# The last column of a ConvFFN: where two ScalarE copies and two VectorE taps stand among the prompt's taps

## The chip, the cores and the metric

The kernel runs on one core of a Trainium2 chip. The metric is the device time of one execution in microseconds; the time of a kernel is the median over its timed executions. A core has five engines that work through queues of their own and meet through semaphores: TensorE (PE, matrix products into PSUM), VectorE (DVE), ScalarE (ACT), GpSimd (POOL) and SyncE (SP, which only issues transfers here). Matrices lie in SBUF and accumulators in PSUM, both 128 partitions wide; large tensors and scratch lie in HBM.

## The reference

One layer of a diffusion backbone on 128 prompt tokens and 1024 sample tokens (a grid of 16 by 64), width 1024: adaLN modulation, a mixer of gated linear attention heads, and a ConvFFN, each with a residual, then a final norm. The change lies in the ConvFFN:

```python
def dw_conv(u, conv_w, conv_b, grid):      # depthwise: 3x3 over the grid, or width 3 over the prompt
    ...
    return out + conv_b

def conv_ffn(h, w_up, conv_w, conv_b, w_down, grid):
    u = dw_conv(h @ w_up, conv_w, conv_b, grid)
    gate, up = jnp.split(u, 2, axis=-1)
    return (jax.nn.silu(gate) * up) @ w_down
```

`w_up` is 1024 x 5632, `w_down` 2816 x 1024, all in float32.

## The kernel before, in words

**Products.** Every float32 operand is split into a high part (a rounded copy, written by ScalarE) and a low part (the rest, a subtraction). One product is then three matmuls: high by high, high by low, low by high. The large products are arranged as seven products of half matrices in place of eight.

**Up stage.** The 2816 hidden channels are 22 columns of 128 (c = 0 to 21), each with a gate half and an up half. For a column PE fills two PSUM tiles `u` (128 channels by 1024 sample tokens, gate and up), and a tile `x` with the prompt's values, which it turns round at the end (`turn_prompt`, L2085). The convolution writes `acc[c][0]` (gate) and `acc[c][1]` (up), 1152 tokens wide: the middle tap with the bias is one ACT instruction for the sample tokens (`conv_middle`, L1964) and one for the prompt (`prompt_middle`, L1994); the other eight taps of the grid (`gate_tap`, `up_tap`, L1982) and the two of the prompt (`prompt_tap`, L2002) are multiply-adds on DVE. Then ACT takes the Silu of the gate (L2131 in the last column), POOL multiplies gate by up (L2172) and the result is stored to the scratch `scr_g`, of which POOL also makes sums (`late`, L1924 to L1928) that are stored to `scr_s`. A column's taps run on DVE while PE works on the next column. Of the last column (c = 21, `last_rest`) three gate taps run inside the loop, and 13 taps of the grid and four of the prompt come behind.

**Down stage.** It is seven products over 11 pairs of columns (j = 0 to 10) each. For a pair, SP loads tokens and weights, 512 columns each, into one raw tile of 128 x 1024 (L129, two transfers), ACT writes the high part (`wuh` or `wh`), and an engine the low part (`wul` or `wl`, a subtraction): in the first product POOL does this for pairs 0 to 6 and DVE for pairs 7 to 10, later DVE for all. A pair is 12 matmuls (four tiles of 128 tokens, three each, L2439); the first three pairs of the first product are taken together, 36 matmuls. Each pair needs both parts; there are seven places for parts and six raw tiles, taken in rotation, so that a place is written again when PE has read it, and a raw tile is loaded again when its low part has been made. In the listings L254 and L133 are the same copy of `load_w`, L254 and L69 the same subtraction; which line is shown depends on who called it.

**What sets the order.** The framework places the instructions on each engine; `tc.issue_after(x)` says that what is made under it stands behind x on its engine. Three chains matter. `vec` strings DVE's taps, prompt taps and the low parts of pairs 7 to 10 one behind the other in the order in which they are written. `InTurn(nc.scalar, "pair_high")` strings ACT's high parts of pairs 1 to 6, starting behind the last column's last copy out of PSUM. `InTurn(nc.gpsimd, "pair_low")` does so for POOL's low parts. An engine executes its queue strictly in order, and SP's loads are a queue too.

Of the kernel before, what the change touches and what calls it, by code (L numbers as in the profile page):

```python
# [49 lines left out]
def kernel(ctx: ExitStack, tc: tile.TileContext, ins, outs, stop=None):  # L50
# [11 lines left out]
    anchor = {}  # L62
# [5 lines left out]
    def split_lo(eng, out, full, hi):  # L68
        return eng.tensor_tensor(out, full, hi.bitcast(F32), op=ALU.subtract)  # L69
# [37 lines left out]
    def turn(key):  # L107
        slots["n"] += 1
        return slots[key][slots["n"] // 2 % len(slots[key])]

    def next_raw():
        slots["raws"].append(slots["raws"].pop(0))
        return slots["raws"][-1]

    def load_w(srcs, shape, eng, high=nc.scalar):

        if slots["fixed"]:
            raw = next_raw()
            hi, lo = slots["fixed"].pop(0)
            slots["fixed"].append((hi, lo))  # L120
        else:
            wp = turn("w")
            raw = turn("raw").tile([P] + shape, F32, name="raw", tag="raw")
            hi = wp["h"].tile([P] + shape, F32R, name="wh", tag="wh")
            lo = wp["l"].tile([P] + shape, F32R, name="wl", tag="wl")
        if isinstance(srcs, (list, tuple)):
            n = shape[-1] // len(srcs)
            for i, src in enumerate(srcs):
                anchor["load"] = nc.sync.dma_start(raw[..., i * n : (i + 1) * n], src)  # L129
        else:  # L130
            anchor["load"] = nc.sync.dma_start(raw, srcs)
        def split():
            high.activation(hi, raw, AF.Copy)  # L133
            split_lo(eng, lo, raw, hi)

        if slots["hold"]:
            slots["held"].append(split)
        else:
            split()
        return hi, lo  # L140
# [122 lines left out]
    def load_pair(p, j):  # L263
        a, b = PRODUCTS[p](j)
        if p > 1:
            return load_w([a, b], [2 * 512], nc.vector)
        low = InTurn(nc.gpsimd, "pair_low") if j < 7 else InTurn(nc.vector, "vec")
        return load_w([a, b], [2 * 512], low, InTurn(nc.scalar, "pair_high") if 0 < j < 7 else nc.scalar)

    def seq_product(p):  # L270
        for j in range(NPAIR):
            seq.append((1, lambda j=j: load_pair(p, j)))
# [1244 lines left out]
    def turn_prompt():  # L1517

        for q in range(2):
            pt = turned["p", q] = ps_p.tile([P, 4, P], F32, name="x", tag="x")  # L1520

            def fn():
                for j in range(4):
                    kt = 4 * q + j
                    last = nc.tensor.transpose(pt[:, j, :], xns[8][:, kt * P : (kt + 1) * P], ident)
                return last

            run("pe", fn)
# [432 lines left out]
    def conv_middle(u, ch, acc, ra=0, rb=NROW):  # L1961

        bc = vcol[:, col["conv_b"] + ch : col["conv_b"] + ch + 1]
        return nc.scalar.activation(  # L1964
            acc[:, ra * GRID : rb * GRID],
            u[:, ra * GRID : rb * GRID],
            AF.Identity,
            bias=bc,
            scale=convc[:, 4 * 44 + ch : 4 * 44 + ch + 1],
        )  # L1970

    def conv_rest(u, ch, acc, ra=0, rb=NROW, part=slice(0, 8)):

        wc = lambda t: convc[:, t * 44 + ch : t * 44 + ch + 1]
        u3 = u.rearrange("p (r c) -> p r c", c=GRID)
        a3 = acc[:, 0:NS].rearrange("p (r c) -> p r c", c=GRID)
        taps = [(dy, dx) for dy in (-1, 0, 1) for dx in (-1, 0, 1) if dy or dx]
        for dy, dx in taps[part]:
            r0, r1 = max(ra, -dy), min(rb, NROW - dy)
            c0, c1 = max(0, -dx), min(GRID, GRID - dx)  # L1980
            o = a3[:, r0:r1, c0:c1]
            last = nc.vector.scalar_tensor_tensor(  # L1982
                o,
                u3[:, r0 + dy : r1 + dy, c0 + dx : c1 + dx],
                wc(3 * (dy + 1) + dx + 1),
                o,
                op0=ALU.mult,
                op1=ALU.add,
            )
        return last  # L1990

    def prompt_middle(pp, ch, acc):
        bc = vcol[:, col["conv_b"] + ch : col["conv_b"] + ch + 1]
        return nc.scalar.activation(  # L1994
            acc[:, NS:NT], pp, AF.Identity, bias=bc, scale=convc[:, 4 * 44 + ch : 4 * 44 + ch + 1]
        )
# [26 lines left out]
    def up(c, p, kts=range(4)):  # L2023

        if p in (2, 3, 5):
            Z, Y = u[c][0][:, 0:512], u[c][0][:, 512:NS]
        else:
            X = u[c][1][:, 0:512]
        chained(
            {  # L2030
                1: lambda: up_product(X, c, "11", "b11", True, False),
                2: lambda: up_product(Z, c, "12", "b21", True, True),
                3: lambda: up_product(Y, c, "s4", "b22", False, True, kts),
                4: lambda: up_product(X, c, "22", "t4", False, True),
                5: lambda: up_product(Y, c, "s1", "t1", True, False),
                6: lambda: up_product(X, c, "s2", "t2", False, False),
                7: lambda: up_product(X, c, "s3", "t3", False, False),
            }[p]
        )
        if p == 5 and c:  # L2040
            copy(c, "p5", Y)
        elif p == 1:
            copy(c, "p1", X)
        elif p == 6:
            copy(c, "u2", X)
# [24 lines left out]
    def vec(fn):  # L2070
        with tc.issue_after(anchor["vec"].ins) if "vec" in anchor else nullcontext():
            anchor["vec"] = fn()

    def gate_tap(c, i):
        vec(lambda: conv_rest(u[c][0], c, acc[c][0], part=slice(i, i + 1)))

    def up_tap(c, i):
        vec(lambda: conv_rest(u[c][1], 22 + c, acc[c][1], part=slice(i, i + 1)))
# [38 lines left out]
    def last_rest(c):  # L2117

        up(c, 4)
        gate_p, up_p = turn_prompt(c)  # L2120
        prompt_middle(*gate_p)
        prompt_middle(*up_p)
        for dx in (-1, 1):
            prompt_tapped(gate_p, dx)
            prompt_tapped(up_p, dx)
        last = conv_middle(u[c][1], 22 + c, acc[c][1])
        with tc.issue_after(last.ins):
            nc.scalar.dma_start(scr_g[c - 1], gs[c - 1])
        for i in range(3, 8):
            gate_tap(c, i)  # L2130
        nc.scalar.activation(acc[c][0], acc[c][0], AF.Silu)  # L2131
        for i in range(8):
            up_tap(c, i)
        second_gate(c)

    def prompt_tapped(pp, dx):
        vec(lambda: prompt_tap(*pp, dx))
# [27 lines left out]
    def second_gate(c):  # L2165

        accg, accu = acc[c]
        if c not in FIXED:
            with after("p1") if c == 0 else nullcontext():
                nc.scalar.activation(accg, accg, AF.Silu)  # L2170
        gs[c] = accg
        last = anchor["gate"] = nc.gpsimd.tensor_tensor(accg, accg, accu, op=ALU.mult)  # L2172
        if c + 1 not in FIXED or c not in FIXED:
            nc.gpsimd.dma_start(scr_g[c], accg)
        if sums_todo and c > 0:
            with tc.issue_after(last.ins):
                sums_todo.pop(0)()
        if c % 2 == 1:
            token_sums(c // 2)
# [7 lines left out]
    for c in range(NHID + 1):  # L2187
# [26 lines left out]
        if c == NHID:  # L2214
            last_rest(c - 1)
        elif c - 1 in FIXED:
            fixed_rest(c - 1)
        elif c > 0:
            taps = prompt_columns(c - 1)
            up(c - 1, 4)  # L2220
            second_half(c - 1)
# [370 lines left out]
```

## Time and profile before

| | |
|---|---|
| three timed executions | 1503.16, 1504.57 and 1507.5 us; median 1504.57 |
| the profiled execution | 1507.08 us, of which the span of the program's instructions is 1505.3 us |
| granted TensorE clock over the span | 0.996 |
| busy in the span | PE 1459.9 us (97%), DVE 1135.9 (75%), ACT 783.1 (52%), POOL 700.6 (47%) |
| the up stage | from about 811 us to 1253.7 us of the span |
| the down stage | from 1253.7 us to the end |

The times in the rows are microseconds from the start of the span. In a row of the timeline stand the start, the duration, the engine (with a q where it is the sequencer that issues a transfer), the line, the operation, what it writes and reads, the shape, and the number of instructions merged in the row; in brackets the idle time ahead of it and what ended that. Neighbouring instructions of one engine overlap by about 0.1 us, so durations of single instructions add up to a little more than the stretch they fill. Matmuls are listed with their full latency (0.39 us), while they start 0.23 us apart.

### The profile page before, as it was taken

Reading aid. Unit: us, or ns where it says so; the run is one execution under the profiler, and the core shown is the slowest. Engines: PE = TensorE matmul, PEld = TensorE weight load, DVE = VectorE, ACT = ScalarE, POOL = GpSimd, SP = SyncE. Lnnn points to the kernel's source line nnn. Section 1 sums busy time; section 2 is a strip of 40 time slices with the busy share of each in tenths; the row PEclk is TensorE's granted clock in tenths of the full one; section 3 lists DMA queues with packets and bytes.
Section 4 is the critical chain, followed back from the end, with each engine's and each line's share of the span. In section 5 each row is a group of like instructions: output and inputs, shape, how many; then the busy total and the mean of one; then the engine's idle time right before and its main releaser. Section 6 shows DMA issues by size and latency. Waiting matters only on the chain.

```text
span 1505.3 us, 31115 instructions
## 1 busy us (share of the span) xinstructions
PE 1459.9 (97%) x12509; PEld 1250.9 (83%) x12509; DVE 1135.9 (75%) x1727; ACT 783.1 (52%) x1524; POOL 700.6 (47%) x524
## 2 busy tenths in 40 slices
PE   6999999999999999899999999999999999999998
PEld 2899998999898999777788888888888887888886
DVE  3766565565565777755799999999999999689475
ACT  3575667555455555622674454444444444466444
POOL 1602122324332241222329999999999996100001
PEclk9999999999999999999999999999999999999999
DMA  9411121335525454867662555545654567979752
GB/s 338 139 44 48 41 61 54 113 91 172 175 77 190 134 165 160 308 238 256 208 193 79 180 166 143 151 115 145 197 134 125 170 167 232 362 257 372 237 192 116
DMA packets 173803, 253.80 MB, mean 169 GB/s; under 512 B 11828, under 2 KB 113698, under 8 KB 171738
## 3 DMA queue, kind: packets, MB, share of 16 engines
q1 hardware_dynamic: 150455, 173.52, 35.9%
q0 software_dynamic: 20000, 66.99, 15.0%
q10 hardware_dynamic: 3203, 11.30, 2.0%
q8 instruction: 98, 1.61, 0.4%
q14 instruction: 47, 0.39, 0.1%
HBM read 191.93 MB, written 82.90 MB: 183 GB/s over the span
## 4 chain that ended last, share of the span: by engine, by line
PE 80%; DMA 6%; DVE 4%; ACT 3%; POOL 3%; issue 3%; SPq 0%; POOLq 0%; DVEq 0%; ACTq 0%
PE u L1798 24%; PE mm L642 15%; PE xb L2439 7%; PE yb L2439 6%; PE mm L656 5%; PE x L2056 4%; PE mm L794 3%; PE lv L981 3%; PE yb L2493 2%; PE u L1562 2%; PE x L1049 2%; PE mm L536 1%; DMA raw<-in_w_in_dram 1%; DMA wa<-in_w_ada_dram 1%; PE ada L1218 1%
## 5 line engine op out<-in xcount | busy, mean ns | idle before, releaser
L1982 DVE SCALAR_TENSOR_TENSOR acc<-u,convc,acc 128x945 f32<-128x945 f32 (+2 forms) x352 | 425.2, 1217 | 6.0
L69 POOL TENSOR_TENSOR wl<-raw,wh 128x1024 fp32r<-128x1024 f32 x40 | 97.8, 2448 | 251.5 <-ACT wh L133 199.0
L642 PE MATMUL mm<-h1h,wh 128*128 128x384 f32 x528 | 185.0, 350 | 0.6 <-ACT qj L545 0.6
L642 PE MATMUL mm<-h1h,wl 128*128 128x384 f32 x528 | 179.0, 339 | 0.0
L642 PE MATMUL mm<-h1l,wh 128*128 128x384 f32 x528 | 179.0, 339 | 0.0
L944 DVE TENSOR_TENSOR Q<-Q,fb 128x384 f32<-128x384 f32 x126 | 82.7, 656 | 85.2 <-PE lv L981 84.4
L69 POOL TENSOR_TENSOR wul<-sr,wuh 128x512 fp32r<-128x512 f32 (+1 forms) x62 | 112.8, 1820 | 11.0 <-ACT wuh L1780 8.4
L69 POOL TENSOR_TENSOR wul<-ra,wuh 128x1024 fp32r<-128x1024 f32 (+1 forms) x43 | 109.1, 2539 | 15.7 <-ACT wuh L1780 15.7
L934 ACT ACTIVATE m<-k 128x384 f32<-128x384 f32 x126 | 70.2, 557 | 82.2 <-DVE k L946 38.7
L2403 POOL TENSOR_TENSOR sq<-sq,mhalf 128x1 f32<-128x1 f32 x9 | 10.8, 1199 | 204.5 <-DVE sq L2402 204.5
L642 PEld LDWEIGHTS mm<-h1h,wh 128*128 128x128 f32 x528 | 99.5, 188 | 5.5 <-issue 3.9
L642 PEld LDWEIGHTS mm<-h1l,wh 128*128 128x128 f32 x528 | 99.5, 188 | 0.6 <-issue 0.2
L642 PEld LDWEIGHTS mm<-h1h,wl 128*128 128x128 f32 x528 | 99.3, 188 | 0.8 <-issue 0.5
L656 PE MATMUL mm<-wh,h1h 128*128 128x256 f32 x288 | 83.9, 291 | 1.5 <-ACT v L681 1.5
L946 DVE TENSOR_TENSOR k<-k,fb 128x384 f32<-128x384 f32 x126 | 74.2, 589 | 12.2 <-ACT m L934 7.2
L656 PE MATMUL mm<-wh,h1l 128*128 128x256 f32 x288 | 80.5, 280 | 0.0
L656 PE MATMUL mm<-wl,h1h 128*128 128x256 f32 x288 | 80.5, 279 | 0.0
L133 ACT ACTIVATE wh<-raw 128x1024 fp32r<-128x1024 f32 x48 | 50.8, 1058 | 42.5 <-PE mm L642 11.8
L2172 POOL TENSOR_TENSOR acc<-acc,acc 128x1152 f32<-128x1152 f32 x22 | 60.5, 2751 | 8.8 <-DVE acc L1982 7.7
L2018 ACT ACTIVATE u2p<-u 128x512 f32<-128x512 f32 x44 | 26.4, 599 | 69.4 <-PE u L1798 68.3
L1780 ACT ACTIVATE wuh<-ra 128x1024 fp32r<-128x1024 f32 (+1 forms) x43 | 44.3, 1034 | 34.6 <-POOL acc L2172 18.4
L1780 ACT ACTIVATE wuh<-sr 128x512 fp32r<-128x512 f32 (+1 forms) x63 | 48.8, 774 | 22.2 <-PE x L2056 16.6
(402 smaller groups left out, 4467.4 us busy)
## 6 DMA issues: line engine op xcount, KB each, us to landing
ra<-in_w_ffn_up_dram SPq DMA_DIRECT2D x84, 256.0 KB, 3.4
raw<-in_w_in_dram SPq DMA_DIRECT2D x32, 512.0 KB, 4.7
v<-in_w_ada_dram SPq DMA_DIRECT2D x27, 512.0 KB, 4.4
scr_s<-late POOLq DMA_DIRECT2D x11, 1024.0 KB, 6.0
scr_t<-in_w_ffn_down_dram POOLq DMA_DIRECT2D x16, 704.0 KB, 8.5
scr_g<-acc ACTq DMA_DIRECT2D x18, 576.0 KB, 3.8
wa<-in_w_ada_dram SPq DMA_DIRECT2D x16, 512.0 KB, 6.2
scr_t<-in_w_ffn_down_dram POOLq DMA_DIRECT2D x2, 2816.0 KB, 12.3
```

Of the source, the lines that this page charges most:

```text
L69: return eng.tensor_tensor(out, full, hi.bitcast(F32), op=ALU.subtract)
L642: anchor["fill"] = mm(ps, a[:, kt, :], h[kt][b], start=(n == 0), stop=(n == 23))
L656: anchor["fill"] = mm(ps, h[kt][t // 3][:, ts_], a[:, kt % 4, :], start=(n == 0), stop=(n == 23))
L934: nc.scalar.activation(aps(t, 0, [[2 * h, NB], [h, 2], [1, h]]), aps(src, 0, [[2 * h, NB], [BL + h, 2], [1, h]]), AF.Copy)
L944: nc.vector.tensor_tensor(qm, qm, aps(ff_, 2 * h - 1, [[BL - h, 2], [2 * h, NB], [0, h]]), op=ALU.mult)
L946: nc.vector.tensor_tensor(km, km, aps(ff_, BL + 2 * h - 1, [[-(BL + h), 2], [2 * h, NB], [0, h]]), op=ALU.mult)
L1780: return lambda: nc.scalar.activation(hi, raw, AF.Copy), lambda eng: split_lo(eng, lo, raw, hi)
L1798: last = mm(dst, w_slot(c, a, x)[:, kt, :], HB[y][b][:, kt, :], start=(start and n == 0), stop=(stop and n == 11), skip_group_check=True,)
L1982: last = nc.vector.scalar_tensor_tensor(o, u3[:, r0 + dy : r1 + dy, c0 + dx : c1 + dx], wc(3 * (dy + 1) + dx + 1), o, op0=ALU.mult, op1=AL ...
L2056: last = mm(pk, HB[h]["p"][:, 4 * half + kt, :], aps(flat(W[x]), a * 512 + kt * P, [[(b - a) * 512, 2], [1, P]]), start=(half + kt + n == ...
L2172: last = anchor["gate"] = nc.gpsimd.tensor_tensor(accg, accg, accu, op=ALU.mult)
L2439: anchor["down"] = mm(banks[i][:, cs], w[a][:, ts_], w[b][:, 512 + cs.start : 512 + cs.stop], start=(start and j == 0 and n == 0), stop=(j ...
```

## The change

Two edits. In `load_pair` the high part of the sixth pair (j = 5), and through the chain that of the seventh, now stands on ACT behind the last column's second prompt middle, where before the chain only ran behind the fifth pair's. In `last_rest` the gate taps 3 and 4 stand ahead of the four prompt taps on DVE, where before they stood behind them. No instruction is added or removed, and no shape changes.

```diff
@@ load_pair
         a, b = PRODUCTS[p](j)
         if p > 1:
             return load_w([a, b], [2 * 512], nc.vector)
+        if j == 5:
+            anchor["pair_high"] = anchor["last_middle"]
         low = InTurn(nc.gpsimd, "pair_low") if j < 7 else InTurn(nc.vector, "vec")
         return load_w([a, b], [2 * 512], low, InTurn(nc.scalar, "pair_high") if 0 < j < 7 else nc.scalar)
@@ last_rest
         gate_p, up_p = turn_prompt(c)
         prompt_middle(*gate_p)
-        prompt_middle(*up_p)
+        anchor["last_middle"] = prompt_middle(*up_p)
+        gate_tap(c, 3)
+        gate_tap(c, 4)
         for dx in (-1, 1):
             prompt_tapped(gate_p, dx)
             prompt_tapped(up_p, dx)
         last = conv_middle(u[c][1], 22 + c, acc[c][1])
         with tc.issue_after(last.ins):
             nc.scalar.dma_start(scr_g[c - 1], gs[c - 1])
-        for i in range(3, 8):
+        for i in range(5, 8):
             gate_tap(c, i)
```

On PE and SP every instruction stands where it stood. The first place is ACT at the turn from the up stage to the down stage: `wh0`, `wh1`, `wh2` are the high parts of pairs 4, 5 and 6, `acc0` and `acc1` up and gate of the last column, L1964 and L1994 the middle taps of the sample tokens and of the prompt, `scr_g20` the store of the column before. Before:

```order
L254 ACTIVATE wh0_14092<-raw0_14098 128x1024
L254 ACTIVATE wh1_14094<-raw1_14099 128x1024
L254 ACTIVATE wh2_14096<-ra_10292 128x1024
L1964 ACTIVATE acc0_9782<-u_13954,vcol_212,convc_8784 128x1024
L1994 ACTIVATE acc1_10299<-x_14037,vcol_212,convc_8784 128x128
L1994 ACTIVATE acc0_9782<-x_14037,vcol_212,convc_8784 128x128
L2128 DMA scr_g20_139<-acc3_10300 128x1152
L2131 ACTIVATE acc1_10299<-acc1_10299 128x1152
```

and in the changed kernel, whose line numbers behind L266 are two to four higher:

```order
L254 ACTIVATE wh0_14092<-raw0_14098 128x1024
L1966 ACTIVATE acc0_9782<-u_13954,vcol_212,convc_8784 128x1024
L1996 ACTIVATE acc1_10299<-x_14037,vcol_212,convc_8784 128x128
L1996 ACTIVATE acc0_9782<-x_14037,vcol_212,convc_8784 128x128
L254 ACTIVATE wh1_14094<-raw1_14099 128x1024
L254 ACTIVATE wh2_14096<-ra_10292 128x1024
L2132 DMA scr_g20_139<-acc3_10300 128x1152
L2135 ACTIVATE acc1_10299<-acc1_10299 128x1152
```

The two high parts and the three middle taps have changed places; the issue of the store now stands behind the high parts.

The second place is POOL in the same stretch, where the low parts `wl0`, `wl1`, `wl2` of pairs 4 to 6 stand beside one of the sums for `scr_s` (`late`). Before:

```order
L254 TENSOR_TENSOR wl0_14093<-raw0_14098,wh0_14092 128x1024
L254 TENSOR_TENSOR wl1_14095<-raw1_14099,wh1_14094 128x1024
L1927 TENSOR_TENSOR late_10480<-acc3_10300 128x512
L254 TENSOR_TENSOR wl2_14097<-ra_10292,wh2_14096 128x1024
L2172 TENSOR_TENSOR acc1_10299<-acc1_10299,acc0_9782 128x1152
```

and in the changed kernel:

```order
L254 TENSOR_TENSOR wl0_14093<-raw0_14098,wh0_14092 128x1024
L1929 TENSOR_TENSOR late_10480<-acc3_10300 128x512
L254 TENSOR_TENSOR wl1_14095<-raw1_14099,wh1_14094 128x1024
L254 TENSOR_TENSOR wl2_14097<-ra_10292,wh2_14096 128x1024
L2176 TENSOR_TENSOR acc1_10299<-acc1_10299,acc0_9782 128x1152
```

The sum has moved ahead of the sixth pair's low part.

The third place is DVE, from the last gate tap that runs inside the loop (the first row) to the first up taps. Before:

```order
L1982 SCALAR_TENSOR_TENSOR acc1_10299<-u_13876,convc_8784,acc1_10299 128x15x63
L2002 SCALAR_TENSOR_TENSOR acc1_10299<-x_14037,convc_8784,acc1_10299 128x127
L2002 SCALAR_TENSOR_TENSOR acc0_9782<-x_14037,convc_8784,acc0_9782 128x127
L2002 SCALAR_TENSOR_TENSOR acc1_10299<-x_14037,convc_8784,acc1_10299 128x127
L2002 SCALAR_TENSOR_TENSOR acc0_9782<-x_14037,convc_8784,acc0_9782 128x127
L1982 SCALAR_TENSOR_TENSOR acc1_10299<-u_13876,convc_8784,acc1_10299 128x16x63 x2
L1982 SCALAR_TENSOR_TENSOR acc1_10299<-u_13876,convc_8784,acc1_10299 128x15x63
L1982 SCALAR_TENSOR_TENSOR acc1_10299<-u_13876,convc_8784,acc1_10299 128x960
L1982 SCALAR_TENSOR_TENSOR acc1_10299<-u_13876,convc_8784,acc1_10299 128x15x63
```

and in the changed kernel:

```order
L1984 SCALAR_TENSOR_TENSOR acc1_10299<-u_13876,convc_8784,acc1_10299 128x15x63
L1984 SCALAR_TENSOR_TENSOR acc1_10299<-u_13876,convc_8784,acc1_10299 128x16x63 x2
L2004 SCALAR_TENSOR_TENSOR acc1_10299<-x_14037,convc_8784,acc1_10299 128x127
L2004 SCALAR_TENSOR_TENSOR acc0_9782<-x_14037,convc_8784,acc0_9782 128x127
L2004 SCALAR_TENSOR_TENSOR acc1_10299<-x_14037,convc_8784,acc1_10299 128x127
L2004 SCALAR_TENSOR_TENSOR acc0_9782<-x_14037,convc_8784,acc0_9782 128x127
L1984 SCALAR_TENSOR_TENSOR acc1_10299<-u_13876,convc_8784,acc1_10299 128x15x63
L1984 SCALAR_TENSOR_TENSOR acc1_10299<-u_13876,convc_8784,acc1_10299 128x960
L1984 SCALAR_TENSOR_TENSOR acc1_10299<-u_13876,convc_8784,acc1_10299 128x15x63
```

The row of two taps, 3 and 4, has moved ahead of the four prompt taps.

## The prediction

> **What bounds the kernel now.** I read the page first (PE busy 97% of the span), then the chain of waits, which runs over PE almost throughout, then what PE waited for from the end of the up stage to the end of the kernel:
>
> ```profile
> PE xb L2439 <- DVE wul L254: 2.2, 1, 2.2
> PE yb L2439 <- DVE e L2388: 0.6, 1, 0.6
> ```
>
> Columns: who waited for whom, microseconds in total, times, longest. In the last 250 us PE waits twice. The change can touch only the first wait. PE's timeline around it:
>
> ```profile
> 1272.64 0.39 PE L2439 MATMUL xb<-wh,wl 128*128 128x512 f32 x1
> 1272.87 0.39 PE L2439 MATMUL xb<-wuh 128*128 128x512 f32 x1
> 1275.46 0.50 PE L2439 MATMUL xb<-wul,wuh 128*128 128x512 f32 x1 [2.21 <-DVE wul L254]
> ...
> 1276.97 0.63 PE L2439 MATMUL xb<-wul,wuh 128*128 128x512 f32 x1
> ...
> 1280.37 0.39 PE L2439 MATMUL xb<-wuh 128*128 128x512 f32 x1
> ...
> 1287.85 0.39 PE L2439 MATMUL yb<-wh 128*128 128x512 f32 x1
> ```
>
> At 1272.87 the eighth pair (j = 7) begins; its second matmul needs the low part, the first that DVE makes, and gets it at 1275.46. From 1276.97 to 1280.37 matmuls take 0.63 us in place of 0.39. The pace without either is 0.227 us, from the chain of waits, where 132 matmuls take 29.92 us:
>
> ```profile
> 1288.01 29.92 PE yb L2439 x132
> ```
>
> Four pairs (j = 7 to 10, 48 matmuls) thus need 48 x 0.2267 = 10.88 us; they took 1287.85 - 1272.87 = 14.98. Lost: 4.10 us, of which 1275.46 - 1273.10 = 2.36 is the wait and 1.74 the slow matmuls. Why DVE is late:
>
> ```profile
> 1250.30 3.68 DVE L1982 SCALAR_TENSOR_TENSOR acc<-u,convc,acc 128x945 f32<-128x945 f32 x3
> 1257.03 1.12 DVE L2002 SCALAR_TENSOR_TENSOR acc<-x,convc,acc 128x127 f32<-128x127 f32 x4 [3.04 <-ACT acc L1994]
> 1258.06 16.22 DVE L1982 SCALAR_TENSOR_TENSOR acc<-u,convc,acc 128x1008 f32<-128x1008 f32 x13
> 1274.20 1.21 DVE L254 TENSOR_TENSOR wul<-ra,wuh 128x1024 fp32r<-128x1024 f32 x1
> 1275.33 5.94 DVE L254 TENSOR_TENSOR wul<-sr,wuh 128x1024 fp32r<-128x1024 f32 x2
> ```
>
> After three gate taps DVE idles 3.04 us for ACT's prompt middles, then runs without a gap to pair 7's low part (1274.20 to 1275.41), and PE starts 0.05 us later. So DVE's idle time is what ends PE's wait. ACT in that stretch:
>
> ```profile
> 1252.25 2.00 ACT L254 ACTIVATE wh<-raw 128x1024 fp32r<-128x1024 f32 x2
> 1254.15 1.05 ACT L254 ACTIVATE wh<-ra 128x1024 fp32r<-128x1024 f32 x1
> 1254.98 0.33 ACTq L2128 DMA_DIRECT2D scr_g<-acc  x1
> 1255.10 1.20 ACT L1964 ACTIVATE acc<-u,vcol,convc 128x1024 f32<-128x1024 f32 x1
> 1256.19 0.80 ACT L1994 ACTIVATE acc<-x,vcol,convc 128x128 f32<-128x128 f32 x2
> 1264.44 1.17 ACT L2131 ACTIVATE acc<-acc 128x1152 f32<-128x1152 f32 x1 [7.45 <-DVE acc L1982]
> ```
>
> **ACT's part.** The middles stand behind three high parts. Their inputs are ready earlier: the end of PE's up column.
>
> ```profile
> 1253.35 0.39 PE L1798 MATMUL u<-t4h,wul 128*128 128x512 f32 x1
> 1253.58 0.38 PE L2085 MATMUL x<-ident,late 128*128 128x128 f32 x2
> ```
>
> `u` is complete at 1253.74, the turned prompt at 1253.96. With `wh1` and `wh2` behind them, ACT is free when `wh0` ends, 1252.25 + about 1.05 = 1253.3. So the sample middle starts at 1253.77 and the prompt middles end 1.9 us later (1255.10 to 1256.99 now), at 1255.7. That is 1.3 us earlier.
>
> **DVE's part.** The two taps need no prompt middle. They run in the idle time: 1253.98 + 2 x 1.25 (16.22 / 13) = 1256.5. There the prompt middles have been ready for 0.8 us. The four prompt taps follow (1258.06 - 1257.03 = 1.03 us), then 11 taps. All of the 3.04 us goes, so every DVE instruction from the 11 taps on shifts by 3.04: pair 7's low part runs from 1271.16 to 1272.38. PE wants it at 1272.87 + 0.23 = 1273.10, so 0.7 us to spare. What is late next is pair 8's low part. SP reloads a raw tile at once when its low part is made, which shows the ends of the single instructions, and POOL's row shows why pair 8's is slow:
>
> ```profile
> 1275.44 0.32 SPq L129 DMA_DIRECT2D ra<-scr_g  x1
> 1279.03 0.32 SPq L129 DMA_DIRECT2D sr<-scr_g  x1
> 1281.30 0.32 SPq L129 DMA_DIRECT2D sr<-scr_g  x1
> 1283.53 0.32 SPq L129 DMA_DIRECT2D raw<-scr_g  x1
> ```
>
> ```profile
> 1274.42 3.50 POOL L2172 TENSOR_TENSOR acc<-acc,acc 128x1152 f32<-128x1152 f32 x1 [7.71 <-DVE acc L1982]
> ```
>
> Pair 8's took 3.7 us (1275.33 to 1279.0) and ended 1.08 us after POOL's gate product (1277.92), about the length of one such instruction: it seems to have stood until POOL was through. POOL's product waits for DVE's last tap, so both shift together and the delay stays. Shifted by 3.04, pair 8 ends at 1275.96, pair 9 at 1278.24, pair 10 at 1280.47. Without the wait PE wants them at 1273.10 + 2.72 per pair: 1275.82, 1278.54, 1281.26. So about 0.15 us of a new wait at pair 8, none behind it. From the next product on DVE was ahead already: at 1290.20 it made the low part of that product's sixth pair (j = 5), which PE wants at 1283.9 + 5 x 2.72 + 0.23 = 1297.7 even when it is four microseconds earlier.
>
> ```profile
> 1290.20 1.21 DVE L69 TENSOR_TENSOR wul<-raw,wuh 128x1024 fp32r<-128x1024 f32 x1
> 1293.73 1.23 DVE L69 TENSOR_TENSOR wul<-raw,wuh 128x1024 fp32r<-128x1024 f32 x1 [2.32 <-ACT wuh L133]
> ```
>
> Its seventh pair's is done at 1294.96, wanted at 1300.4. The loads behind these also move, since most are released by DVE; unmoved they would still do.
>
> **POOL, SP and the store.** What stands behind the moved instructions:
>
> ```profile
> 1257.96 5.13 POOL L254 TENSOR_TENSOR wl<-raw,wh 128x1024 fp32r<-128x1024 f32 x2
> 1262.68 1.66 POOL L1927 TENSOR_TENSOR late<-acc 128x512 f32<-128x512 f32 x1
> 1263.94 2.78 POOL L254 TENSOR_TENSOR wl<-ra,wh 128x1024 fp32r<-128x1024 f32 x1
> ```
>
> ```profile
> 1260.76 0.33 SPq L129 DMA_DIRECT2D raw<-scr_g  x1
> ```
>
> `wh1` and `wh2` now end at about 1256.6 and 1257.6, 2.4 us later, but POOL takes up `wl1` only after 1260.3. The sum ahead of it costs 1.26 us (1262.68 to 1263.94): `wl1` ends at 1264.4 in place of 1263.1, `wl2` at 1266.7 as before. PE wants them at 1267.65 and 1270.37 (24 and 12 matmuls ahead of pair 7, and one), so 3.3 and 3.7 us to spare: cost nothing, one raw reload 1.3 us later. The store of `scr_g20` is issued at 1257.5, not 1254.98. Pair 10's load at 1260.76 waits for it. How long transfers that touch `scr_g` take to land, and the loads of `raw` from it:
>
> ```profile
> DMA to landing us min/median/max: 1.9/2.9/10.0
> ...
> raw<-scr_g SPq DMA_DIRECT2D x6, 256.0 KB, 4.6
> ```
>
> With 2.9 the store lands at 1260.4, with 10.0 at 1267.5, and SP's queue would stand for 6.7 us. Pair 10's high part is wanted at 1281.0. A load takes 4.6 us, ACT 1.05: even then it is ready at about 1273.2. Nothing, with bounds of 0 on both sides. The Silu follows tap 7 and moves 3 us ahead, and so do the high parts behind it.
>
> **The slow matmuls.** Stretches of one length, PE's busy time first, the granted clock third from the end:
>
> ```profile
> 386.05:389.46 3.41, 1.88 (x61) 1.15 (x59) 0.00 (x0) 0.47 (x1) 1.00 (x1) 1.00 0.57 157
> 628.39:631.81 3.42, 1.59 (x54) 1.12 (x54) 2.91 (x9) 2.16 (x8) 0.05 (x1) 1.00 1.02 413
> 631.81:635.22 3.41, 3.41 (x25) 2.37 (x28) 2.04 (x6) 2.43 (x6) 1.50 (x2) 0.50 1.01 407
> 1273.51:1276.93 3.42, 1.47 (x6) 1.24 (x7) 3.42 (x3) 0.00 (x0) 2.51 (x1) 1.00 0.38 128
> 1276.93:1280.34 3.41, 3.41 (x9) 2.67 (x8) 3.41 (x2) 1.06 (x1) 3.01 (x4) 0.50 0.63 239
> ```
>
> Twice a stretch of 3.41 us in which PE idled 53 to 57% is followed by one at half the clock; one with 45% idle (386.05) shows none. I take it that the wait brings the half clock, and without the wait the 1.74 us goes too. The Trainium skill ("TensorE: Matmul & The Clock Gate", section "Why this matters for your kernels") puts the limit at idle gaps of more than about 3 us; by it 2.2 us would bring no half clock and 1.74 us would stay. The row of 1276.93 speaks against it.
>
> **The sum,** against the profiled execution (1507.08): -2.36 + 0.15 - 1.74 = -3.95, so 1503.1. The median of the timed executions is 2.5 below that execution, so it had less of such losses. If the 3.41 us grid lies anywhere, 2.21 us of idle time puts half a window (1.71) into one with (1.20 + 2 x 0.50) / 3.41 = 65% of its positions. For a typical execution I count 0.65 x 1.74 = 1.1, in all -2.2 - 1.1 = -3.3: 1504.57 - 3.3 = 1501.2. A change under 0.3% (4.5 us) is about what a measurement here cannot tell from none.
>
> **The rivals.**
> 1. The half clock has another cause, or was not in the median execution: only the wait goes, -2.2, so 1502.4. For it: the median is 2.5 us below the profiled time. Against it: the rows above. The skill's rule belongs here.
> 2. POOL's product starts ahead of pair 7's low part and DVE stands behind it. Both are released by the same tap; now DVE is 0.22 us ahead (1274.20 against 1274.42). The other way round the low part ends at 1271.3 + 2.7 + 1.1 = 1275.1, PE still waits 2.0 us, the half clock stays: about -0.3, so 1504.3. That POOL's product took 3.50 us here speaks for such blocking, but the order is by the tap's end, and stays. The Trainium skill ("SBUF — State Buffer", "SBUF: two separate sides") has it that whichever of the two starts first keeps the port for its whole instruction.
> 3. The change doesn't do what it says: the middles are not earlier (ACT held by something else). Then the taps alone fill 2.5 of the 3.04 us, DVE shifts by 2.5, pair 7 is in time still and pair 8 0.7 us late: -1.7 - 1.1, 1501.8. Within the forecast's range.
> 4. Slower: the store. From a landing after 1281.0 - 4.6 - 1.05 = 1275.3 (18 us after issue) on, pair 10's high part is late and PE waits microsecond for microsecond. To lose the gain of 3.3 and 4.5 us more it must land at about 1283, 26 us after issue: 1509.1 and more. Against it: the longest was 10.0 us.
>
> **How the numbers follow.** Forecast 0.75 (with rival 3, 0.06 of it), rival 1 0.13, rival 2 0.08, rival 4 0.04. The forecast's saving lies between 2.2 and 3.95, so 1500.6 to 1502.4; the three timed executions lie 4.3 us apart, a median of three scatters by some 1.5 us, so its own range is 1498.4 to 1503.4. The range takes in part of rival 2: 1498.2 to 1504.0. Faster by over 0.3% means below 1500.06, 1.1 below the forecast: some 0.4 of the forecast, 0.15 of rival 1, in all 0.32. Slower by over 0.3%: rival 4, 0.04. Within: 0.64.
>
> **What would show it.** Right: no idle time on DVE ahead of the prompt taps; the second matmul of pair 7 0.23 us after the first; at most 0.3 us of waiting at pair 8; the clock 1.00 through this stretch; `yb` starting at about 1283.9. Wrong: pair 7 or 8 waiting for DVE by a microsecond or more (rival 2), or a wait for ACT at pairs 5 or 6, or SP standing long at the load of `scr_g20`; a half-clock window without a wait ahead of it (rival 1).

## The result, and the profile after

| | before | changed |
|---|---|---|
| median | 1505.85 us (22 executions, 1502.66 to 1507.94) | 1502.06 us (22 executions, 1499.41 to 1505.68) |
| span of the profiled execution | 1505.3 us | 1499.6 us |

The ratio is 0.998 with a 95% interval of 0.9974 to 0.9986: 2.1 to 3.9 us of 1505.85. That is a small gain: its interval is clear of 1, but its size stays under the 0.3% (4.5 us) that was named as about what a measurement can tell. The forecast was a saving of 3.3 us and 1501.2 us. Between the two medians the saving is 3.79 us, 0.5 more than forecast; the time came out 0.9 above the forecast all the same, because the median of before, from which it was counted, was 1504.57 with three executions and is 1505.85 with 22.

What TensorE waited for from the end of the up stage on (who for whom, microseconds in total, times, longest), in the changed kernel:

```profile
PE yb L2443 <- DVE e L2392: 0.6, 1, 0.6
```

The wait of 2.2 us for VectorE's `wul` is gone from the list. PE's timeline at the eighth and ninth pair (j = 7 and 8) and at the start of the next product:

```profile
1271.04 0.39 PE L2443 MATMUL xb<-wuh 128*128 128x512 f32 x1
1271.27 0.39 PE L2443 MATMUL xb<-wul,wuh 128*128 128x512 f32 x1
...
1273.76 0.39 PE L2443 MATMUL xb<-wuh 128*128 128x512 f32 x1
1274.14 0.50 PE L2443 MATMUL xb<-wul,wuh 128*128 128x512 f32 x1
1274.48 0.39 PE L2443 MATMUL xb<-wuh,wul 128*128 128x512 f32 x1
...
1282.22 0.39 PE L2443 MATMUL yb<-wh 128*128 128x512 f32 x1
```

Pair 7's second matmul follows 0.23 us after the first. At pair 8 the step is 0.38 us, a wait of 0.15, and the next step 0.34: the matmul after a late one starts 0.11 us late as well. No matmul takes 0.63 us. DVE in that stretch:

```profile
1248.49 6.29 DVE L1984 SCALAR_TENSOR_TENSOR acc<-u,convc,acc 128x945 f32<-128x945 f32 x5
1254.70 1.11 DVE L2004 SCALAR_TENSOR_TENSOR acc<-x,convc,acc 128x127 f32<-128x127 f32 x4
1255.73 13.62 DVE L1984 SCALAR_TENSOR_TENSOR acc<-u,convc,acc 128x945 f32<-128x945 f32 x11
1269.26 1.22 DVE L254 TENSOR_TENSOR wul<-ra,wuh 128x1024 fp32r<-128x1024 f32 x1
1270.40 3.69 DVE L254 TENSOR_TENSOR wul<-sr,wuh 128x1024 fp32r<-128x1024 f32 x1
```

Five gate taps, four prompt taps and 11 taps follow one another, and no row has idle time in brackets. ACT:

```profile
1252.00 1.21 ACT L1966 ACTIVATE acc<-u,vcol,convc 128x1024 f32<-128x1024 f32 x1 [0.52 <-issue]
1253.11 0.45 ACT L1996 ACTIVATE acc<-x,vcol,convc 128x128 f32<-128x128 f32 x1
1253.18 0.33 ACTq L2132 DMA_DIRECT2D scr_g<-acc  x1
1253.45 0.46 ACT L1996 ACTIVATE acc<-x,vcol,convc 128x128 f32<-128x128 f32 x1
1253.79 1.07 ACT L254 ACTIVATE wh<-raw 128x1024 fp32r<-128x1024 f32 x1
1259.51 1.17 ACT L2135 ACTIVATE acc<-acc 128x1152 f32<-128x1152 f32 x1 [3.71 <-DVE acc L1984]
```

The prompt middles end at 1253.91, 0.8 us ahead of the prompt taps. So that profiles can be compared whose earlier stages differ, the rest counts a loss L: the time from pair 7's first matmul to the first matmul of `yb`, less the 10.88 us that 48 matmuls take. Before, L was 14.98 - 10.88 = 4.10 us; in the changed kernel it is 1282.22 - 1271.04 - 10.88 = 0.30. Where the 5.6 us between the two spans (1505.27 and 1499.64, unrounded) lie: 3.81 in the stretch from the first `xb` matmul to the first of `yb` (34.14 us before, 30.33 now), 1.82 ahead of it (it begins at 1253.71 before, at 1251.89 now), in stages that the change does not touch. Behind it both have 210.36 us from the first `yb` matmul to the last matmul.

### The profile page after: what moved, and what is told of

Same layout as the page of the kernel before. It is cut to its first block, busy times and chain, and to the rows that moved or that the text cites. A ratio compares the mean times of both kernels' runs of the same rounds, so it can differ in the third digit from the quotient of the medians.

```text
span 1499.6 us, 31115 instructions
## 1 busy us (share of the span) xinstructions
PE 1459.5 (97%) x12509; PEld 1250.8 (83%) x12509; DVE 1137.3 (76%) x1727; ACT 782.8 (52%) x1524; POOL 700.2 (47%) x524
## 4 chain that ended last, share of the span: by engine, by line
PE 84%; DMA 4%; DVE 4%; ACT 3%; POOL 2%; issue 2%; SPq 0%; POOLq 0%; ACTq 0%; DVEq 0%
PE u L1800 25%; PE mm L644 15%; PE xb L2443 8%; PE mm L658 6%; PE yb L2443 6%; PE x L2058 4%; PE mm L796 3%; PE lv L983 3%; PE yb L2497 2%; PE u L1564 2%; PE x L1051 2%; PE mm L538 1%; DMA raw<-in_w_in_dram 1%; DMA wa<-in_w_ada_dram 1%; PE ada L1220 1%
## 5 line engine op out<-in xcount | busy, mean ns | idle before, releaser
L946 DVE TENSOR_TENSOR Q<-Q,fb 128x384 f32<-128x384 f32 x126 | 85.7, 680 | 84.7 <-PE lv L983 83.8
```

What stands on the lines that cost most here:

```text
L946: nc.vector.tensor_tensor(qm, qm, aps(ff_, 2 * h - 1, [[BL - h, 2], [2 * h, NB], [0, h]]), op=ALU.mult)
```

## The experiments

The theory: what counts is when VectorE delivers the low parts of pairs 7 and 8. The rivals: one of the two edits carries the gain; both are needed; the gain comes from the Silu, the high parts and the loads being earlier; only the wait at pair 7 counts; the half clock has another cause.

| run | L, us | waits of PE, us | median, us | ratio to before, 95% |
|---|---|---|---|---|
| ScalarE edit alone | 2.19 | 0.96 (pair 7), 0.58 (pair 8) | 1504.08 | 0.9993 (0.9984 to 1.0001) |
| VectorE edit alone | 0.81 | 0.50 (pair 8) | 1502.03 | 0.9983 (0.9973 to 0.9994) |
| before, pair 7's low part on GpSimd | 0.69 | 0.39 (pair 9) | 1503.18 | 0.9986 (0.9977 to 0.9996) |
| changed, pair 7's low part on GpSimd | 0.00 | none | 1501.69 | 0.9977 (0.9968 to 0.9987) |
| changed, one tap more | 1.52 | 0.29 (pair 7), 0.60 (pair 8) | 1502.08 | 0.9976 (0.9967 to 0.9986) |
| changed, four taps more | 6.66 | 3.87 (pair 7) | 1507.16 | 1.0013 (1.0004 to 1.0022) |
| changed, gate product late on VectorE | 0.00 | none | 1502.12 (one execution) | |
| before, once more | 3.44 | 2.21 (pair 7), 0.56 (pair 8) | 1506.81 (one execution) | |

The waits are those in the brackets of PE's rows. They begin when the matmul ahead has ended, some 0.2 us after the late one could have started, so L is larger than their sum; L is the price.

### The ScalarE edit alone

```diff
+        if j == 5:
+            anchor["pair_high"] = anchor["last_middle"]
...
-        prompt_middle(*up_p)
+        anchor["last_middle"] = prompt_middle(*up_p)
```

> The ScalarE edit alone (sixth and seventh pair's high parts behind the prompt middles; the gate taps 3 and 4 stay behind the prompt taps). I count the loss L: the time from pair 7's first matmul to the first matmul of yb, less 10.88 us (48 matmuls); before 4.10, changed kernel 0.30. Theory: VectorE's arrival at the low parts of pairs 7 and 8 sets L. The prompt middles end 1.3 us earlier than before, so VectorE still idles 1.7 us ahead of the prompt taps, the low parts are 1.3 us earlier than before and 1.75 later than in the changed kernel: L about 2.0, split over a wait at pair 7 (about 1.0) and one at pair 8 (about 0.9), and no half-clock window, since no window is half idle. Time about 1.3 to 2.2 us under before. Rival (the ScalarE edit carries the gain): L about 0.3, time as the changed kernel, 3 to 4 us under before. Rival (both edits are needed): L about 4, time as before.

DVE's row at the prompt taps, and PE's late matmuls:

```profile
1253.29 1.12 DVE L2004 SCALAR_TENSOR_TENSOR acc<-x,convc,acc 128x127 f32<-128x127 f32 x4 [1.77 <-ACT acc L1996]
```

```profile
1270.39 0.39 PE L2441 MATMUL xb<-wuh 128*128 128x512 f32 x1
1271.73 0.50 PE L2441 MATMUL xb<-wul,wuh 128*128 128x512 f32 x1 [0.96 <-DVE wul L254]
1275.35 0.50 PE L2441 MATMUL xb<-wul,wuh 128*128 128x512 f32 x1 [0.58 <-DVE wul L254]
1283.46 0.39 PE L2441 MATMUL yb<-wh 128*128 128x512 f32 x1
```

DVE idles 1.77 us in place of 3.04, and L is 1283.46 - 1270.39 - 10.88 = 2.19. The two waits are where the theory has them. This edit alone does not carry the gain; by the timing its own effect cannot be told from none (0.9984 to 1.0001).

### The VectorE edit alone

```diff
         prompt_middle(*up_p)
+        gate_tap(c, 3)
+        gate_tap(c, 4)
...
-        for i in range(3, 8):
+        for i in range(5, 8):
```

> The VectorE edit alone (gate taps 3 and 4 ahead of the prompt taps; ScalarE's order as before). Theory: the two taps fill 2.5 of the 3.04 us of idle time, VectorE idles about 0.5 us ahead of the prompt taps, the low parts come 0.5 us later than in the changed kernel: L about 0.8 (pair 7 without a wait or nearly, pair 8 about 0.6 to 0.7), no half clock; time 2.5 to 3.3 us under before, within 0.6 us of the changed kernel. Rival (the ScalarE edit carries the gain): L about 4, time as before.

```profile
1254.84 1.12 DVE L2002 SCALAR_TENSOR_TENSOR acc<-x,convc,acc 128x127 f32<-128x127 f32 x4 [0.45 <-ACT acc L1994]
```

```profile
1270.69 0.39 PE L2441 MATMUL xb<-wuh 128*128 128x512 f32 x1
1274.29 0.50 PE L2441 MATMUL xb<-wul,wuh 128*128 128x512 f32 x1 [0.50 <-DVE wul L254]
1282.38 0.39 PE L2441 MATMUL yb<-wh 128*128 128x512 f32 x1
```

DVE idles 0.45 us and L is 1282.38 - 1270.69 - 10.88 = 0.81, 0.51 above the changed kernel. This edit alone brings most of the gain: 3.29 of the 3.80 us between the two profiles. Its median (1502.03) can't be told from the changed kernel's. So the edits are not both needed; the ScalarE edit, which alone brings 1.91, adds 0.51 on top of this one, since both fill the same 3.04 us. These shares count from the profile of before with a half-clock stretch (4.10); from the other one, below (3.44), they are 2.63 and 1.25 of 3.14.

### The same relief without either edit

The kernel before, with pair 7's low part on GpSimd, which idles there, ahead of the last column's gate product:

```diff
-        low = InTurn(nc.gpsimd, "pair_low") if j < 7 else InTurn(nc.vector, "vec")
+        low = InTurn(nc.gpsimd, "pair_low") if j < 8 else InTurn(nc.vector, "vec")
...
+        if j == 7:
+            with after("pair_low"):
+                hooks["second_gate"](NHID - 1)
...
-        second_gate(c)
```

> The kernel before, neither edit; pair 7's low part is made by GpSimd, which idles there, ahead of the last column's gate product. VectorE keeps its 3.04 us of idle time and ends the last tap as late as before. Theory (only the low parts' arrival matters, not the idle time itself): pair 7's low part is ready about 5 us early; pair 8's is then VectorE's first and ends where pair 7's ended, 0.4 us ahead of need; pair 9's stands behind GpSimd's gate product and is about 0.5 us late: L about 0.6, no half clock, time 2.7 to 3.5 us under before. Rival (the gain came from the earlier Silu, high parts and loads): L stays near 3 to 4.

```profile
1257.35 1.12 DVE L2008 SCALAR_TENSOR_TENSOR acc<-x,convc,acc 128x127 f32<-128x127 f32 x4 [3.02 <-ACT acc L2000]
1258.39 16.22 DVE L1988 SCALAR_TENSOR_TENSOR acc<-u,convc,acc 128x1008 f32<-128x1008 f32 x13
1274.53 4.83 DVE L254 TENSOR_TENSOR wul<-sr,wuh 128x1024 fp32r<-128x1024 f32 x2
```

DVE's idle time stays (3.02 us) and the last tap is as late as before; L falls to 0.69 all the same. So most of the gain comes without filling the idle time and without an earlier Silu or earlier loads: what counts is the deadline of the low parts. The order of some later loads on SP's queue changed with this edit too, which no wait shows.

The changed kernel with the same edit:

> The changed kernel, with pair 7's low part on GpSimd as well. Theory: no low part is late any more, L about 0.0 to 0.2, no wait of TensorE at all between the up stage and yb; time 0.1 to 0.3 us under the changed kernel, which a timing can't resolve. Rival (another engine takes over as the bound, GpSimd or the loads): L above 0.5.

PE waits for nothing in the stretch and L is 0.00. By the profile this beats the changed kernel by 0.30 us. Its median is 0.4 us lower, which its interval (0.9968 to 0.9987, against 0.9974 to 0.9986) doesn't resolve.

### VectorE made late again

The changed kernel, with more instructions of the taps' form that add zero times `u`, between the last tap and pair 7's low part (the second run has `range(4)`):

```diff
             up_tap(c, i)
+        au = acc[c][1][:, 0:960]
+        for _ in range(1):
+            vec(
+                lambda: nc.vector.scalar_tensor_tensor(
+                    au, u[c][1][:, 64:1024], 0.0, au, op0=ALU.mult, op1=ALU.add
+                )
+            )
         second_gate(c)
```

> The changed kernel with one more VectorE instruction of the taps' form, that adds zero times u to acc, between the last tap and pair 7's low part: every low part 1.25 us later. Theory: pair 8 is the limit, so L grows by the full 1.25, from 0.30 to about 1.55, about 0.5 at pair 7 and the rest at pair 8, without a half clock; time 1.2 us above the changed kernel. Rival (pair 7's wait alone counts, as in the prediction's sum): pair 7 has 0.7 us to spare, so L grows by about 0.5 only.

```profile
1269.75 1.16 DVE L2141 SCALAR_TENSOR_TENSOR acc<-u,acc 128x960 f32<-128x960 f32 x1
```

The instruction took 1.16 us and L grew by 1.22, from 0.30 to 1.52. The full delay arrives at PE, and not only the 0.5 us by which pair 7 would be late: pair 8 is the limit. The timing does not show it (1502.08 us against 1502.06 of the changed kernel, which was timed apart from it): 1.2 us is below what ten or twenty executions resolve.

> The same with four such instructions, 5.0 us. Theory: TensorE idles 4.2 us at pair 7, so a half-clock window follows for certain, and by its slowed matmuls pair 8 is no longer waited for: L about 4.3 + 1.7 = 6.0, time 5.7 us above the changed kernel. Rival (the half clock is not brought by the wait): no window of half clock near there, L about 5.3 (4.3 at pair 7, 0.9 at pair 8).

Stretches of one length, PE's busy time first, the granted clock third from the end:

```profile
1269.00:1272.41 3.41, 1.03 (x5) 0.53 (x3) 3.31 (x4) 0.00 (x0) 0.00 (x0) 1.00 0.50 183
1272.41:1275.82 3.41, 1.91 (x5) 1.53 (x6) 3.41 (x3) 0.00 (x0) 2.96 (x1) 0.50 0.25 67
1275.82:1279.23 3.41, 3.41 (x10) 2.64 (x9) 3.41 (x2) 1.06 (x1) 3.01 (x4) 0.50 0.69 230
1279.23:1282.64 3.41, 3.41 (x16) 2.80 (x15) 3.41 (x3) 0.00 (x0) 3.33 (x2) 1.00 0.96 311
```

The four took 4.73 us; L is 6.66 where 6.0 was expected. The half clock came, and for two stretches and not one: the first stretch is 70% idle, the second, with PE still waiting for 1.5 us of it, runs at half clock and is followed by another. The median is 5.1 us above the changed kernel's and above before's, with an interval clear of 1. So a delay of VectorE alone undoes the whole gain and more.

### GpSimd's product out of the way

The changed kernel, with the last column's gate product made by VectorE behind pair 10's low part:

```diff
-        second_gate(c)
+    def last_gate(c):
+        accg, accu = acc[c]
+        gs[c] = accg
+        vec(lambda: nc.vector.tensor_tensor(accg, accg, accu, op=ALU.mult))
+        nc.gpsimd.dma_start(scr_g[c], accg)
+        token_sums(c // 2)
...
+        if j == NPAIR - 1:
+            hooks["last_gate"](NHID - 1)
```

> The changed kernel with the last column's gate product made by VectorE behind pair 10's low part, not by GpSimd beside the low parts. Theory (VectorE's subtractions and GpSimd's product block each other): GpSimd is idle then, pair 8's low part takes 1.2 us in place of 3.7, as do those of pairs 9 and 10 (1.2 in place of 2.3), no wait at pair 8. Rival (pair 8's low part is slow for its own sake): 3.7 us as before.

```profile
1270.22 1.22 DVE L254 TENSOR_TENSOR wul<-ra,wuh 128x1024 fp32r<-128x1024 f32 x1
1271.35 2.35 DVE L254 TENSOR_TENSOR wul<-sr,wuh 128x1024 fp32r<-128x1024 f32 x2
1273.62 1.22 DVE L254 TENSOR_TENSOR wul<-raw,wuh 128x1024 fp32r<-128x1024 f32 x1
1274.76 1.35 DVE L2147 TENSOR_TENSOR acc<-acc,acc 128x1152 f32<-128x1152 f32 x1
```

```profile
1277.07 4.74 POOL L1931 TENSOR_TENSOR late<-acc,acc 128x512 f32<-128x512 f32 x1
```

The same low parts and the same sum in the changed kernel:

```profile
1270.40 5.96 DVE L254 TENSOR_TENSOR wul<-sr,wuh 128x1024 fp32r<-128x1024 f32 x2
1276.28 2.30 DVE L254 TENSOR_TENSOR wul<-raw,wuh 128x1024 fp32r<-128x1024 f32 x1
1273.96 1.31 POOL L1926 TENSOR_TENSOR late<-acc,acc 128x512 f32<-128x512 f32 x1
```

Pairs 8 and 9 together take 2.35 us in place of 5.96, pair 10 takes 1.22 in place of 2.30, and L is 0.00. So pair 8's 3.69 us are 1.2 of work and 2.5 of standing behind GpSimd's product. It goes both ways: the first sum on GpSimd, which took 1.31 us in the changed kernel, now falls among VectorE's subtractions and takes 4.74: 3.4 us of standing, as long as nearly three of them. The Trainium skill ("SBUF — State Buffer", section "Who interferes with whom") states this: a VectorE instruction with two inputs in SBUF and a GpSimd instruction that reads SBUF exclude each other for whole instructions. The rows agree.

### The kernel before, once more

> The kernel before, once more, for a second look at the stall. The half-clock grid may lie otherwise. If half of a window is idle again: half clock, L about 4.1, no wait at pair 8. If not: the clock stays 1.00, and pair 8 is waited for by about 0.85 us (its low part ends 3.57 us behind pair 7's, TensorE takes 2.72 for a pair): L about 3.25, so that the half clock would cost 0.85 us net and not 1.74.

```profile
1273.28 0.39 PE L2439 MATMUL xb<-wuh 128*128 128x512 f32 x1
1275.88 0.50 PE L2439 MATMUL xb<-wul,wuh 128*128 128x512 f32 x1 [2.21 <-DVE wul L254]
1279.49 0.50 PE L2439 MATMUL xb<-wul,wuh 128*128 128x512 f32 x1 [0.56 <-DVE wul L254]
1287.60 0.39 PE L2439 MATMUL yb<-wh 128*128 128x512 f32 x1
```

```profile
1271.52:1274.93 3.41, 2.15 (x10) 1.45 (x8) 3.34 (x4) 0.35 (x1) 0.09 (x1) 1.00 0.83 226
1274.93:1278.34 3.41, 2.46 (x11) 2.00 (x12) 3.41 (x2) 0.00 (x0) 3.41 (x1) 1.00 0.46 151
```

The same wait of 2.21 us, this time split over two stretches (37% and 28% idle), and no half clock. The grid is laid through a half-clock stretch of the same profile at 483.05, 231 steps earlier. Now pair 8 is waited for, which in the first profile it was not, and L is 1287.60 - 1273.28 - 10.88 = 3.44. Between the two profiles of before the half clock thus makes 0.66 us, and not 1.74: PE, slowed, came to pair 8 after its low part; at full speed it comes too early and waits.

## Why the prediction held, and where its sum was wrong

- **What bounds.** Right. DVE's 3.04 us of idle time, through the low parts, was what PE waited for. Making DVE late by 1.16 and 4.73 us brought the loss back; relieving DVE of pair 7 took most of it away (L 0.69) with the idle time in place.
- **ACT's part.** Right: the prompt middles ended 2.02 us after the first `xb` matmul (1251.89 to 1253.91), forecast 1255.7 - 1253.71 = 2.0; 3.28 before.
- **DVE's part.** Right: pair 7's low part began 17.37 us after that matmul, forecast 1271.16 - 1253.71 = 17.45; 20.49 before.
- **What is late next.** Right in place and size: 0.15 us at pair 8. The 0.11 us behind a late matmul were not in the sum; L is 0.30.
- **POOL.** Nothing showed, as forecast: `wl1` and `wl2` began 7.90 and 10.27 us after the first `xb` matmul, no wait for them.
- **The store.** Wrong, without a price: it was not issued at 1257.5 but at 1253.18, 1.29 us after the first `xb` matmul (1.27 before). ACT's sequencer issues it while three instructions that stand ahead of it have still to run; the row of before, 1254.98, ahead of the middles that it stands behind, had shown that. So "strictly in order" holds here for the instructions that ACT executes and not for the issue of a store. The later issue on which rival 4 rests did not happen. What the prediction had right is that pair 10's load stands behind this store. What SP waited for between 1250 and 1275 us in the changed kernel (who for whom, microseconds in total, times, longest) holds this row:

```profile
SPq L129 <- DMA scr_g<-acc: 1.5, 1, 1.5
```

The load was issued at 1259.36, 7.47 us after the first `xb` matmul where before it was 7.05: 0.4 us later, and PE did not wait for it.

- **The slow matmuls.** The mechanism was right, the term "-1.74" was mis-sized. I took the half clock's cost as what goes when it goes. But the kernel before has a second wait behind it, at pair 8, that the half clock hid; without half clock it is paid. By these profiles the change saves 3.44 - 0.30 = 3.14 us where there is no half clock and 3.80 where there is, not 2.2 to 3.95. Both lie inside the measured 2.1 to 3.9. With the share of 65%, which was worked out and not measured, it is 3.6. The sum's 3.3 came close by luck: the wait was counted too low (2.2 for 3.1) and the half clock too high (1.1 for 0.4), and the two errors nearly cancel.
- **The half clock's cause.** Three profiles bear on it: 57% idle in one stretch brought it, 70% brought it, the same wait split 37 and 28% did not. 2.21 us were enough when most of them fell into one stretch. By the limit of about 3 us that the Trainium skill gives ("TensorE: Matmul & The Clock Gate", "Why this matters for your kernels") this wait would not have brought it; the measurement decides. The idle share of one stretch is not the whole rule either. In the kernel before:

```profile
10.59:14.00 3.41, 1.59 (x7) 0.27 (x3) 0.94 (x6) 2.13 (x4) 0.56 (x1) 1.00 1.01 392
14.00:17.42 3.42, 1.94 (x11) 0.85 (x12) 2.07 (x8) 2.71 (x6) 0.76 (x2) 1.00 1.02 358
34.48:37.90 3.42, 1.90 (x13) 0.95 (x14) 2.44 (x8) 3.17 (x7) 3.10 (x3) 1.00 1.06 378
37.90:41.31 3.41, 3.41 (x13) 3.31 (x12) 3.41 (x2) 3.41 (x7) 3.41 (x2) 0.50 1.03 413
```

A stretch 53% idle was not followed by half clock, and one 44% idle was (with other shapes of matmul than here). So the limit of half a stretch, on which the 65% rests, is not shown, and neither is what else decides.

- **"The median had less of such losses".** Not borne out. The second profile of before had no half clock here and still took 1506.81 us. In all ten profiles the time from the first `yb` matmul to the last is 210.35 or 210.36 us, and the first `xb` matmul comes at 1250.49 to 1254.13 us. Much of the scatter that I meant to explain with this stretch thus arises ahead of it.
- **Range and chances.** 1502.06 lies in 1498.2 to 1504.0 and within 0.3% of before, the likeliest of the three cases. The inner range of 1498.4 to 1503.4 does not follow from its terms: 1500.6 to 1502.4, widened by 1.5 on both sides, is 1499.1 to 1503.9.

Open: why the start of the down stage scatters by 3.6 us, with the same instructions in the stages ahead of it. The three profiles with the latest starts (1253.71, 1254.13, 1254.05) are the two of before and the one built on it with neither edit, while the seven with an edit start at 1250.49 to 1252.86; whether the edits have a part in that is not shown. The medians do not ask for a second effect: the difference in L, 3.14 to 3.80 us, lies inside the measured 2.1 to 3.9.

## What to carry to other kernels

When a wait is to be removed, follow every consumer behind it at full pace: a second deadline (here pair 8's low part) may sit just behind the first, hidden by the slowdown that the first one brings, and then sets what each microsecond is worth. Idle time on a supplying engine is worth what it costs at that engine's next deadline, and the cheapest remedy may be to fill the gap with work that is ready (the two taps alone brought 3.29 of the 3.80 us between the profiles) or to hand the urgent piece to an engine that idles.

## What the runs showed of the hardware

- A wait of one length, 2.21 us, came with a loss of 3.44 or 4.10 us by where it fell on a grid of 3.41 us: 57% of one stretch idle, or 37 and 28% of two. A half-clock stretch that is itself 44% idle (1.91 us busy of 3.41) was followed by another at half clock, while a full-clock stretch 45% idle (386.05 in the kernel before) was not. Among the stretches 44 to 54% idle at full clock in the two profiles of before some were followed by half clock (34.48 and 628.39) and some were not (10.59 and 386.05).
- After a late matmul the next one starts 0.34 us later in place of 0.23, in every profile with a wait at full clock.
- VectorE's subtractions and GpSimd's product or sums hold each other up: 3.69 us for 1.2 of work on the one, 4.74 for 1.31 on the other, which is longer than one whole subtraction.
- A transfer's issue on ScalarE's queue runs ahead of instructions that stand in front of it: at 1253.18, while three of these ended at 1253.91, 1254.86 and 1255.80.
